# A hybrid attention/SSD kernel: one transfer per bias table, 2 KB stretches for the cumulative sums, no margin for late row sums

## The chip, the cores and the metric

The kernel runs on one core of a Trainium2 chip. The metric is the device time of one execution in microseconds (us), lower is better. Three executions of the kernel before took 1742.33, 1743.96 and 1747.86 us; the median is 1743.96 us. In the profile PE is the matrix engine (TensorE), PEld its weight loads, DVE the VectorE, ACT the ScalarE, POOL the GpSimd, and SP the engine whose queue issues nearly all DMA transfers. SPq, ACTq, DVEq mean the instruction queue of that engine.

## The reference, cut to what matters

The reference is a backbone of two layers over 256 latent tokens and 256 context tokens of width 2048, all in float32. Layer 0 joins 16 heads of neighbourhood attention with 32 heads of a bidirectional state-space scan (SSD); layer 1 is a gated short convolution. The parts that the change touches:

```python
s_lat = einsum('bqhd,bkhd->bhqk', qr, kb) * scale + bias      # bias = rpb gathered per head
s_lat = where(mask, s_lat, -inf)
...
cs = cumsum(dtc * a, axis=1)                 # a row of 128 sums per chunk, head and direction
decay = exp(where(tri, cs[:, :, None] - cs[:, None, :], -inf))
w = cb[..., None] * decay * dtc[:, None]
y = y + einsum('bign,bgrpn->bigrp', cc, h) * exp(cs)[..., None]
...
m = silu(cond) @ w + b                       # adaln: shift, scale, gate of each layer
```

The first 4096 columns of layer 0's modulation matrix are needed at once. Its last 2048 columns (the gate) and all 6144 of layer 1's are needed later; these are the "late row sums" below: 64 column blocks of 128, each in two halves of 1024 rows, so 128 products of a 128x1024 tile with a vector, each summed along its rows.

## The kernel before, in words

All large products run on PE in split precision. A weight tile of 128x1024 floats (512 KB) is loaded from DRAM into one of the `raw` buffers; ACT rounds it to its high half H (`split`, L422), DVE subtracts to get the low half Lo (`low_part`, L429), and PE multiplies act_H·H, act_H·Lo and act_L·H (`mm`, L196). There are three places for split tiles during layer 0. A tile is used up in 24 matmuls of 256 columns, or 12 or 24 of 512. PE transposes are L200.

The order of every engine's instructions is worked out while the program is built, by a planner (`Plan`, L38) that keeps a clock for each engine (`plan.t`), a ready time for each stretch of memory, and fixed costs. A DMA issue costs it 450 ns of the issuing engine; a transfer's end on the SP queue is 1000 ns, plus its bytes at 270 bytes per ns behind the transfer before, plus 1000 ns (2500 in place of the last 1000 for a transfer issued by ACT). For a DRAM tile it keeps ready times in units of 256 floats over the whole stretch from the first to the last element (`keys`, L50). Around the stream of matmuls, generators (tasks) wait in three lists, `urgent`, `side` and `back`, with horizons of 4500, 2500 and 1500 ns. Before each group of matmuls `pump` (L279) asks `may` (L247) of each task whether its next step can be put in now. For a DVE step the planner's DVE clock must be at most the horizon past PE's, and the data ready at most 400 ns past the later of the two; a step of the `back` list adds 2000 ns to the ready time first (L264).

The parts that the change touches:

- `head_gen` (L1134), one task per attention head. Its bias table of 128 rows lands in one of two tiles `bias[hd % 2]`, by three DMAs on the SP queue (L1140): 128, 64 and 128 columns at offsets 0, 304 and 544. DVE adds the window mask to the three pieces (L1146). The first score block reads columns 0 to 207 and 128 to 335, the second 336 to 543 and 464 to 671 (L1163), with zeros between, written once by POOL (L994).
- `dt_gen` (L1264) makes the cumulative sums of 64 rows (32 heads, two directions) of 256. ACT's queue writes them to DRAM as `csr` and their exponentials as `exr` (L1352, L1353), each [64, 256], direction-major. `make_x` (L1418) reads `exr` back spread over 64 partitions (L1482), `group_gen` (L1502) `csr` over 128 partitions (L1523). A head's row is two stretches of 1 KB, 32 rows apart.
- `gemv_gen` (L872), a `back` task, does the 128 late row sums. Their tiles (`in_adaT`) are loaded into `raw` buffers beside the weight tiles by `issue` (L367, the DMA at L383), at most one or two at a time. Each is one DVE instruction (L885) against `csb`, a vector spread over all partitions (L879, loaded six times). A sum is only put in when its tile is planned to be ready 1500 ns before the planner's DVE clock (L881). The sum frees the buffer, and `issue` puts the next load on the SP queue. After 32, 96 and 128 sums `n_back` rises to 3, 11.5 and 15; layer 0's residual waits for the first, layer 1's input for the second, the output for the third.

SP's queue, like each engine's, runs in the order in which the planner put its instructions; an instruction that waits holds those behind it.

Of the kernel before, what the change touches and what calls it, by code (L numbers as in the profile page):

```python
# [141 lines left out]
def kernel(ctx: ExitStack, tc, x, cx, ada0, w0, adaT, w_in, w_out, sc_in, sc_out, rpb, small, const,  # L142
# [7 lines left out]
    V, S, G, T, DMA = nc.vector, nc.scalar, nc.gpsimd, nc.tensor, nc.sync  # L150
    DMA2 = nc.scalar
    plan = Plan()
    E = plan.add
# [4 lines left out]
    def drt(shape, name):  # L158
        return dr.tile(list(shape), F32, name="dram_" + name)
# [683 lines left out]
    def dot_gen():  # L843
# [8 lines left out]
        for j in DOTS:  # L852
# [16 lines left out]
            E(V.tensor_tensor(out=S_, in0=S_, in1=P_("ab0")[:, k2].unsqueeze(2).to_broadcast([128, 2, 2]), op=ALU.add))  # L869
            got.add(("S", j))  # L870

    def gemv_gen():  # L872
        yield from rows_out(csil, crow.rearrange("r (b c) -> (r b) c", c=128), 32)
        got.add("crow")
        yield when(lambda: ("S", DOTS[-1]) in got)
        for q, blocks in enumerate(GEM):
            for h in range(2):
                yield W_("SP", crow, csb)
                E(DMA.dma_start(csb, crow[0, h * 1024:(h + 1) * 1024].partition_broadcast(128)))  # L879
                for m in blocks:  # L880
                    yield when(lambda: ("gem", m, h) in RAW and plan.ready([RAW["gem", m, h][0]]) + 1500 <= plan.t["DVE"])  # L881
                    yield W_("DVE", RAW["gem", m, h][0], csb)
                    raw, _ = RAW.pop(("gem", m, h))
                    ngem[0] -= 1
                    E(V.tensor_tensor_reduce(out=raw, in0=raw, in1=csb, scale=1.0, scalar=0.0, op0=ALU.mult, op1=ALU.add,  # L885
                                             accum_out=gp[:, h, m:m + 1]))
                    give_raw(raw)
                    issue()
            yield W_("DVE", gp)
            p2 = lambda lo, n: (gp[:, 0, lo:lo + n], gp[:, 1, lo:lo + n])  # L890
            if q == 1:
                a, b = p2(16, 32)
                o = M1.rearrange("p r b -> p (r b)")
                E(V.tensor_tensor(out=o, in0=a, in1=b, op=ALU.add))
                E(V.tensor_tensor(out=o, in0=o, in1=P_("ab1")[:, 0:32], op=ALU.add))
            else:
                a, b = p2(0 if q == 0 else 48, 16)
                E(V.tensor_tensor(out=a, in0=a, in1=b, op=ALU.add))
                E(V.tensor_tensor(out=a, in0=a, in1=P_("ab0" if q == 0 else "ab1")[:, 32:48], op=ALU.add))
                yield from rows_out(a, in_rows(mrow[q // 2]))  # L900
            n_back[0] = (3, 11.5, 15)[q]
# [89 lines left out]

    vd = drt([256, 512], "vd")
    for b_ in bias:
        E(G.memset(b_.rearrange("p a b -> p (a b)")[:, 128:544], 0.0))  # L994
    dcol = P_("dcol")


# [136 lines left out]
    def head_gen(a, h):  # L1134
# [1 line left out]
        bt, s4 = bias[hd % 2], s4s[hd % 4]  # L1136
        yield when(lambda: hd < 2 or ("pv", hd - 2) in got)
        yield W_("SP")
        bf = bt.rearrange("p a b -> p (a b)")[:, :672]
        for o_, c_, n_ in ((0, 0, 128), (304, 128, 64), (544, 192, 128)):  # L1140
            E(DMA.dma_start(bf[:, o_:o_ + n_], rpb[hd, :, c_:c_ + n_]))
        yield W_("DVE", bt)
        for o_, m_ in ((0, mask[:, 0:32]), (304, mid), (544, mask[:, 32:64])):
            n_ = m_.shape[-1]
            bv = bf[:, o_:o_ + 4 * n_].rearrange("p (c r) -> p c r", r=4)
            E(V.tensor_tensor(out=bv, in0=bv, in1=m_.unsqueeze(2).to_broadcast([128, n_, 4]), op=ALU.add))  # L1146
# [12 lines left out]
        def top(qt, ps):  # L1159
            sp = sps[qt] = tmp()  # L1160
            if qt == 0:
                E(V.memset(sp[:, 416:480], 0.0))
            b_ = bass.AP(tensor=bf.tensor, offset=bf[:, 336 * qt:].offset, ap=[bf.ap[0], [128, 2], [1, 208]])  # L1163
            sc = sp[:, span(qt)]
            E(V.tensor_tensor_reduce(out=two(sc), in0=two(ps[:, :416]), in1=b_, scale=1.0,
                                     scalar=-3.0e38, op0=ALU.add, op1=ALU.max, accum_out=s4[:, qt:qt + 1]))
            give(free_b, ps)
            E(V.tensor_scalar(out=s4[:, 2 + qt:3 + qt], in0=s4[:, qt:qt + 1], scalar1=-1.0, scalar2=None, op0=ALU.mult))
            yield W_("ACT", sp, s4)
            E(S.activation(sc, sc, AF.Exp, bias=s4[:, 2 + qt:3 + qt], scale=1.0, accum_out=s4[:, 4 + qt:5 + qt]))  # L1170
# [88 lines left out]

    dtl, csl, wst, wl = st([128, 2, 64], "dtl"), st([128, 2, 64], "csl"), st([128, 2, 64], "wst"), st([128, 64], "wl")  # L1260
    ncs, ebc = st([128, 2, 64], "ncs"), st([128, 64], "ebc")
    csr, exr = drt([64, 256], "csr"), drt([64, 256], "exr")

    def dt_gen(ps):  # L1264
        f, b = slice(0, 32), slice(32, 64)
# [83 lines left out]
        E(S.activation(rw[:64, 256:512], pr[:64, :256], AF.Exp))  # L1349
        give(free_b, pr)  # L1350
        yield W_("AQ", rw)
        E(DMA2.dma_start(csr, rw[:64, 0:256]))  # L1352
        E(DMA2.dma_start(exr, rw[:64, 256:512]))  # L1353
        give(free_t, rw)
        got.add("dt")

# [61 lines left out]
    def make_x(s, gi, ps):  # L1418
# [11 lines left out]
        if True:  # L1430
# [45 lines left out]
            for b in range(2):  # L1476
                i = 2 * gi + b
                yield W_("SP", exr)
                Et = tmp()
                for hh in range(2):  # L1480
                    e0 = exr[4 * g + 2 * b + hh, :]
                    E(DMA.dma_start(two(Et)[64 * hh:64 * hh + 64],  # L1482
                                    bass.AP(tensor=e0.tensor, offset=e0.offset, ap=[[0, 64], [32 * 256, 2], [1, 256]])))
                yield W_("PE", h1t, nb=1)
                pin = bank()
                for d_ in range(2):
                    for c in range(2):
                        hs = h0t if c == d_ else h1t
                        mm(pin[:, d_ * 256 + c * 128:d_ * 256 + (c + 1) * 128], hs[:, d_ * 256 + b * 128:d_ * 256 + (b + 1) * 128],
                           Cl[:, gi, c * 128:(c + 1) * 128], d_ == 0 and c == 0, True)  # L1490
                yield W_("DVE", pin, Et)
                E(V.tensor_tensor(out=Et, in0=pin, in1=Et, op=ALU.mult))
                give(free_b, pin)
                yield W_("DVE", Et)
                E(V.scalar_tensor_tensor(out=yi[:, i, :], in0=xf[b][:, 0:256], scalar=dcol[:, 4 * s + i:4 * s + i + 1],
                                         in1=Et[:, 0:256], op0=ALU.mult, op1=ALU.add))
                E(V.tensor_tensor(out=yi[:, i, :], in0=yi[:, i, :], in1=Et[:, 256:512], op=ALU.add))
                give(free_t, Et, xf[b])
# [3 lines left out]
    def group_gen(s, gi):  # L1502
# [14 lines left out]
        for b in range(2):  # L1517
            yield W_("SP", csr)
            rows = []
            for hh in range(2):  # L1520
                rw = tmp()
                r0 = csr[4 * g + 2 * b + hh, :]
                E(DMA.dma_start(two(rw), bass.AP(tensor=r0.tensor, offset=r0.offset, ap=[[0, 128], [32 * 256, 2], [1, 256]])))  # L1523
                rows.append(rw)
            for hh in range(2):
                h = 4 * g + 2 * b + hh
                rw = rows[hh]
                Dm, M = rw[:, 0:256], rw[:, 256:512]
                yield W_("ACT", rw)
                for c in range(2):  # L1530
                    cc = slice(c * 128, (c + 1) * 128)
                    E(S.activation(M[:, cc], M[:, cc], AF.Identity, bias=ncs[:, c, 32 + h:33 + h], scale=1.0))
                yield W_("DVE", M)
                for c in range(2):
                    cc = slice(c * 128, (c + 1) * 128)
                    E(V.scalar_tensor_tensor(out=Dm[:, cc], in0=Dm[:, cc], scalar=csl[:, c, h:h + 1], in1=M[:, cc],
                                             op0=ALU.subtract, op1=ALU.min))
                yield W_("ACT", Dm)
                E(S.activation(Dm, Dm, AF.Exp))
                for c in range(2):  # L1540
                    cc = slice(c * 128, (c + 1) * 128)
                    E(S.activation(M[:, cc], CB[:, 256 + c * 128:256 + (c + 1) * 128], AF.Copy,
                                   scale=dtl[:, c, 32 + h:33 + h]))
                yield W_("DVE", M)
                for c in range(2):
                    cc = slice(c * 128, (c + 1) * 128)
                    E(V.scalar_tensor_tensor(out=M[:, cc], in0=CB[:, cc], scalar=dtl[:, c, h:h + 1], in1=M[:, cc],  # L1547
                                             op0=ALU.mult, op1=ALU.add))
                yield W_("DVE", M, Dm)

                o = rows[0][:, hh * 256:hh * 256 + 256]
                E(V.tensor_tensor(out=o, in0=Dm, in1=M, op=ALU.mult))
                Ds.append(o)
            give(free_t, rows[1])
            if b:
                give(free_t, CB)
            both_rows.append(rows[0])
# [656 lines left out]
```

## Time and profile before

| what | value |
|---|---|
| median of three executions | 1743.96 us (1742.33 to 1747.86) |
| the profiled execution | 1743.12 us, of which its span is 1741.3 us |
| instructions | 24796 |
| ACT, DVE busy | 776.8 us (45%), 1251.3 us (72%) |
| PE granted clock | 0.999 of full speed |
| moved by DMA | 390.52 MB in 198872 packets, 224 GB/s on average |
| packets under 512 B, under 2 KB | 18712, 58456 |

The page of the profile gives the busy time of each engine, the chain of work that ended last, the costliest groups of instructions and the DMA issues with their time from issue to landing. A group's row reads: line, engine, operation, out<-in, count, then busy us and mean ns. The view of waits gives, for an engine and line, what ended its idle time: total us, number of times, longest. The table of windows gives busy us of each engine per stretch of the span, with the number of instructions, the granted clock of PE, the share of the 16 DMA engines' time that was busy, and GB/s.

### The profile page before, as it was taken

Reading aid. Unit: us, or ns where it says so; the run is one execution under the profiler, and the core shown is the slowest. Engines: PE = TensorE matmul, PEld = TensorE weight load, DVE = VectorE, ACT = ScalarE, POOL = GpSimd, SP = SyncE. Lnnn points to the kernel's source line nnn. Section 1 sums busy time; section 2 is a strip of 40 time slices with the busy share of each in tenths; the row PEclk is TensorE's granted clock in tenths of the full one; section 3 lists DMA queues with packets and bytes.
Section 4 is the critical chain, followed back from the end, with each engine's and each line's share of the span. In section 5 each row is a group of like instructions: output and inputs, shape, how many; then the busy total and the mean of one; then the engine's idle time right before and its main releaser. Section 6 shows DMA issues by size and latency. Waiting matters only on the chain.

```text
span 1741.3 us, 24796 instructions
## 1 busy us (share of the span) xinstructions
PE 1718.7 (99%) x9237; PEld 1450.3 (83%) x9237; DVE 1251.3 (72%) x2106; ACT 776.8 (45%) x1367; POOL 33.9 (2%) x28
## 2 busy tenths in 40 slices
PE   6999999999999999999999999999999999999998
PEld 4777988888888889888888898888888888888887
DVE  5698788867575878475878587887667667676754
ACT  5434544445243445243435243665445344444442
POOL 0000100001000001000001000000000000000000
PEclk9999999999999999999999999999999999999999
DMA  9987644676654765654776567757867878787863
GB/s 360 373 325 271 206 134 150 195 210 195 201 170 140 229 205 180 205 170 139 229 208 199 177 196 235 249 195 258 292 209 246 280 258 266 263 282 257 286 214 113
DMA packets 198872, 390.52 MB, mean 224 GB/s; under 512 B 18712, under 2 KB 58456, under 8 KB 198496
## 3 DMA queue, kind: packets, MB, share of 16 engines
q1 hardware_dynamic: 191472, 382.35, 67.5%
q10 hardware_dynamic: 7280, 6.59, 1.1%
q8 instruction: 72, 1.18, 0.3%
q14 instruction: 48, 0.39, 0.1%
HBM read 379.27 MB, written 9.62 MB: 223 GB/s over the span
## 4 chain that ended last, share of the span: by engine, by line
PE 94%; DMA 3%; DVE 2%; ACT 0%; issue 0%; SPq 0%; POOL 0%; DVEq 0%; ACTq 0%
PE bank L196 91%; PE bank L200 3%; DMA raw<-in_ada 1%; DMA tmp<-dram_mixd 1%; DMA csb<-dram_crow 1%; DVE w L429 0%; DMA bias<-in_rpb 0%; DVE csb L859 0%; DVE raw L885 0%; DVE mix L1704 0%; DVE tmp L1547 0%; SPq L603 0%; SPq L383 0%; DVE raw L859 0%; DVE bias L1146 0%
## 5 line engine op out<-in xcount | busy, mean ns | idle before, releaser
L422 ACT CAST w<-raw 128x1024 fp32r<-128x1024 f32 (+1 forms) x344 | 360.0, 1048 | 550.2 <-PE bank L196 415.6
L429 DVE TENSOR_TENSOR w<-raw,w 128x1024 fp32r<-128x1024 f32 (+1 forms) x344 | 416.7, 1215 | 246.3 <-ACT w L422 244.0
L196 PE MATMUL bank<-hH,w 128*128 128x256 f32 (+1 forms) x2064 | 485.6, 324 | 1.3 <-DVE w L429 1.3
L196 PE MATMUL bank<-w,hH 128*128 128x512 f32 x1280 | 406.0, 396 | 3.3 <-ACT hH L780 2.5
L196 PEld LDWEIGHTS bank<-hH,w 128*128 128x128 f32 x2064 | 344.6, 188 | 33.9 <-DVE w L429 1.9
L196 PE MATMUL bank<-hL,w 128*128 128x256 f32 (+1 forms) x1040 | 334.3, 321 | 0.0
L196 PEld LDWEIGHTS bank<-w,hH 128*128 128x128 f32 x1280 | 238.1, 189 | 55.1 <-ACT hH L780 3.0
L196 PE MATMUL bank<-w,hL 128*128 128x512 f32 x640 | 249.9, 391 | 0.2
L196 PEld LDWEIGHTS bank<-hL,w 128*128 128x128 f32 x1040 | 196.4, 189 | 14.7
L196 PE MATMUL bank<-w,h 128*128 128x512 f32 x768 | 178.5, 389 | 0.0
L196 PEld LDWEIGHTS bank<-w,h 128*128 128x128 f32 x768 | 143.9, 188 | 29.8
L885 DVE CUSTOM_DVE_ANT_0 raw<-raw,csb 128x1024 f32<-128x1024 f32 x128 | 154.9, 1216 | 0.3 <-DMA csb<-dram_crow 0.3
L196 PEld LDWEIGHTS bank<-w,hL 128*128 128x128 f32 x640 | 120.4, 188 | 25.9 <-DVE hL L792 0.9
L196 PE MATMUL bank<-w,mix 128*128 128x512 f32 x588 | 138.7, 392 | 0.6 <-DVE w L429 0.4
L196 PEld LDWEIGHTS bank<-w,mix 128*128 128x128 f32 x588 | 109.4, 188 | 23.5 <-DVE w L429 0.8
L1367 DVE SCALAR_TENSOR_TENSOR tmp<-bank,cwh,tmp 128x508 f32<-128x508 f32 (+1 forms) x96 | 71.2, 745 | 1.9
L196 PE MATMUL bank<-KL,h 128*128 128x512 f32 x264 | 63.8, 389 | 0.0
L429 DVE TENSOR_TENSOR KL<-raw,KL 128x1024 fp32r<-128x1024 f32 x32 | 39.1, 1223 | 28.2 <-ACT KL L422 28.0
L196 PEld LDWEIGHTS bank<-KL,h 128*128 128x128 f32 x264 | 49.5, 188 | 10.2
L196 PE MATMUL bank<-QT,h 128*128 128x512 f32 x168 | 55.6, 390 | 0.0
L196 PE MATMUL bank<-wH,h 128*128 128x512 f32 x168 | 55.3, 389 | 0.0
L429 DVE TENSOR_TENSOR wL<-raw,wH 128x1024 fp32r<-128x1024 f32 x31 | 37.9, 1222 | 20.6 <-ACT wH L422 20.6
(306 smaller groups left out, 1956.1 us busy)
## 6 DMA issues: line engine op xcount, KB each, us to landing
raw<-in_w_in SPq DMA_DIRECT2D x196, 512.0 KB, 3.8
raw<-in_adaT SPq DMA_DIRECT2D x128, 512.0 KB, 4.8
raw<-in_sc_in SPq DMA_DIRECT2D x128, 512.0 KB, 5.0
raw<-in_w_out SPq DMA_DIRECT2D x64, 512.0 KB, 4.6
raw<-in_ada SPq DMA_DIRECT2D x35, 512.0 KB, 8.0
raw<-in_sc_out SPq DMA_DIRECT2D x32, 512.0 KB, 4.4
raw<-in_w SPq DMA_DIRECT2D x16, 512.0 KB, 5.6
tmp<-dram_csr SPq DMA_DIRECT2D x32, 256.0 KB, 6.3
```

Source lines behind the costliest of these rows:

```text
L196: E(T.matmul(o, l, r, start=start, stop=stop, skip_group_check=True))
L200: E(T.transpose(o, i, ident if k == 128 else ident[:k, :k]))
L422: E(S.copy(H, v))
L429: E(V.tensor_tensor(out=Lo, in0=v, in1=H.bitcast(F32), op=ALU.subtract))
L885: E(V.tensor_tensor_reduce(out=raw, in0=raw, in1=csb, scale=1.0, scalar=0.0, op0=ALU.mult, op1=ALU.add, accum_out=gp[:, h, m:m + 1]))
L1367: E(V.scalar_tensor_tensor(out=do, in0=di, scalar=cwh[:, 32 * k + ch:32 * k + ch + 1], in1=do, op0=ALU.mult, op1=ALU.add))
```

## The change

It has three parts.

1. The bias table in DRAM becomes [16, 128, 3, 128]: the middle piece is padded with 64 zero columns, and one DMA brings the three pieces of 128 columns to offsets 0, 304 and 608 (192 KB a head in place of 160 KB in three DMAs). The zero fill reaches to column 608, and the second score block reads its two pieces 192 apart in place of 128.
2. `csr` and `exr` become [32, 2, 256], so that a head's two rows are one stretch of 512 floats (2 KB). ACT's queue writes each with two DMAs, one per direction; the 64 reads take one stretch per partition.
3. The late row sums are counted (`n_dot`). While fewer are done than the planner's PE clock divided by 9600 ns, less 22, the condition of 1500 ns is waived; the data must still meet the general rule for a `back` step.

```diff
@@ gemv_gen
+    n_dot = [0]
...
-                    yield when(lambda: ("gem", m, h) in RAW and plan.ready([RAW["gem", m, h][0]]) + 1500 <= plan.t["DVE"])
+                    yield when(lambda: ("gem", m, h) in RAW and (n_dot[0] < plan.t["PE"] / 9600.0 - 22 or plan.ready([RAW["gem", m, h][0]]) + 1500 <= plan.t["DVE"]))
...
+                    n_dot[0] += 1
...
-        E(G.memset(b_.rearrange("p a b -> p (a b)")[:, 128:544], 0.0))
+        E(G.memset(b_.rearrange("p a b -> p (a b)")[:, 128:608], 0.0))
@@ head_gen
-        bf = bt.rearrange("p a b -> p (a b)")[:, :672]
-        for o_, c_, n_ in ((0, 0, 128), (304, 128, 64), (544, 192, 128)):
-            E(DMA.dma_start(bf[:, o_:o_ + n_], rpb[hd, :, c_:c_ + n_]))
+        bf = bt.rearrange("p a b -> p (a b)")[:, :736]
+        E(DMA.dma_start(bass.AP(tensor=bf.tensor, offset=bf.offset, ap=[bf.ap[0], [304, 3], [1, 128]]), rpb[hd]))
...
-        for o_, m_ in ((0, mask[:, 0:32]), (304, mid), (544, mask[:, 32:64])):
+        for o_, m_ in ((0, mask[:, 0:32]), (304, mid), (608, mask[:, 32:64])):
...
-            b_ = bass.AP(tensor=bf.tensor, offset=bf[:, 336 * qt:].offset, ap=[bf.ap[0], [128, 2], [1, 208]])
+            b_ = bass.AP(tensor=bf.tensor, offset=bf[:, 336 * qt:].offset, ap=[bf.ap[0], [128 + 64 * qt, 2], [1, 208]])
@@ dt_gen
-    csr, exr = drt([64, 256], "csr"), drt([64, 256], "exr")
+    csr, exr = drt([32, 2, 256], "csr"), drt([32, 2, 256], "exr")
...
-        E(DMA2.dma_start(csr, rw[:64, 0:256]))
-        E(DMA2.dma_start(exr, rw[:64, 256:512]))
+        for d_ in range(2):
+            E(DMA2.dma_start(csr[:, d_, :], rw[32 * d_:32 * d_ + 32, 0:256]))
+        for d_ in range(2):
+            E(DMA2.dma_start(exr[:, d_, :], rw[32 * d_:32 * d_ + 32, 256:512]))
@@ make_x
-                    e0 = exr[4 * g + 2 * b + hh, :]
-                    E(DMA.dma_start(two(Et)[64 * hh:64 * hh + 64],
-                                    bass.AP(tensor=e0.tensor, offset=e0.offset, ap=[[0, 64], [32 * 256, 2], [1, 256]])))
+                    e0 = exr[4 * g + 2 * b + hh]
+                    E(DMA.dma_start(Et[64 * hh:64 * hh + 64], e0.rearrange("d t -> (d t)").partition_broadcast(64)))
@@ group_gen
-                r0 = csr[4 * g + 2 * b + hh, :]
-                E(DMA.dma_start(two(rw), bass.AP(tensor=r0.tensor, offset=r0.offset, ap=[[0, 128], [32 * 256, 2], [1, 256]])))
+                r0 = csr[4 * g + 2 * b + hh]
+                E(DMA.dma_start(rw, r0.rearrange("d t -> (d t)").partition_broadcast(128)))
@@ kernel (host)
-    table = np.concatenate([pick(0, kc[:32]), pick(0, kc[32:40]), pick(1, kc[24:32]), pick(1, kc[32:])], axis=2)
+    table = np.concatenate([pick(0, kc[:32]), pick(0, kc[32:40]), pick(1, kc[24:32]), np.zeros((16, 128, 64), np.float32),
+                            pick(1, kc[32:])], axis=2).reshape(16, 128, 3, 128)
```

## The prediction

> **What bounds the kernel now.** I read the page's busy line and chain of waits first, then a table of windows over the whole span, then the list of what PE waited for after 200 us.
>
> ```profile
> span 1741.3 us, 24796 instructions
> PE 1718.7 (99%) x9237; PEld 1450.3 (83%) x9237; DVE 1251.3 (72%) x2106; ACT 776.8 (45%) x1367; POOL 33.9 (2%) x28
> PE 94%; DMA 3%; DVE 2%; ACT 0%; issue 0%; SPq 0%; POOL 0%; DVEq 0%; ACTq 0%
> ```
>
> ```profile
> core 0: us, PE busy (x) PEld busy (x) DVE busy (x) ACT busy (x) POOL busy (x), PEclk, DMA share, GB/s
> 0.00:50.00 50.00, 35.38 (x264) 24.70 (x265) 29.21 (x88) 30.61 (x69) 3.18 (x10) 0.97 0.95 367
> 50.00:200.00 150.00, 148.67 (x902) 114.84 (x901) 116.76 (x195) 65.01 (x134) 2.65 (x1) 1.00 0.83 298
> 200.00:400.00 200.00, 200.00 (x1195) 176.21 (x1195) 158.99 (x310) 93.84 (x192) 4.44 (x3) 1.00 0.59 177
> 400.00:410.00 10.00, 8.68 (x72) 8.32 (x71) 8.00 (x18) 8.20 (x34) 4.50 (x2) 1.00 0.73 215
> 410.00:1100.00 690.00, 690.00 (x3926) 599.81 (x3925) 498.29 (x895) 289.41 (x558) 16.14 (x9) 1.00 0.62 192
> 1100.00:1115.00 15.00, 14.42 (x63) 11.40 (x62) 11.58 (x28) 9.74 (x21) 0.00 (x0) 1.00 0.67 228
> 1115.00:1736.00 621.00, 621.00 (x2825) 514.94 (x2825) 427.06 (x574) 279.95 (x364) 3.02 (x4) 1.00 0.75 247
> 1736.00:1741.30 5.30, 0.51 (x3) 0.08 (x1) 1.38 (x2) 0.00 (x0) 0.00 (x0) 0.98 0.13 49
> ```
>
> ```profile
> PE bank L196 <- DVE w L429: 1.7, 2, 1.3
> ```
>
> PE is the bound from 50 us to the end, at a granted clock of 1.00. It is idle 14.62 us in the first 50 us, 1.33 up to 200 us, 1.32 at 400 to 410, 0.58 at 1100 to 1115, and 4.79 in the tail while the last results go out. Nothing else is missing. The change's first transfers start at 219.7 us (the bias row below), and it leaves the tail's work as it is, so **all that it can win is 1.32 + 0.58 = 1.90 us**, plus pauses too short to show behind pipelined matmuls. The chain's 3% of DMA is no prize: the chain runs through a transfer from where PE paused, while PE was busy beside it. So the question is what becomes of two pauses, and whether new ones come.
>
> **The pause at 404 us.** The timeline around it, rows of SP, ACT, DVE and PE:
>
> ```profile
> 391.96 0.93 SPq L1523 DMA_DIRECT2D tmp<-dram_csr  x2
> 394.02 4.86 SPq L1141 DMA_DIRECT2D bias<-in_rpb  x6
> ...
> 397.67 0.70 ACT L1532 ACTIVATE tmp<-tmp,ncs 128x128 f32<-128x128 f32 x2 [2.03 <-DMA tmp<-dram_csr]
> 402.21 1.12 ACT L422 CAST w<-raw 128x1024 fp32r<-128x1024 f32 x1
> ...
> 401.60 1.21 DVE L1146 TENSOR_TENSOR bias<-bias,const 128x128 f32<-128x128 f32 x6 [1.04 <-DMA bias<-in_rpb]
> 403.94 1.22 DVE L429 TENSOR_TENSOR w<-raw,w 128x1024 fp32r<-128x1024 f32 x1
> ...
> 405.21 0.50 PE L196 MATMUL bank<-hH,w 128*128 128x256 f32 x2 [1.32 <-DVE w L429]
> ```
>
> Two heads' tables come by six issues in 4.86 us (0.81 each); the last lands at 401.6. DVE stood 1.04 us for it; the mask (L1146), a row sum and then the low half (L429) follow, and PE stands 1.32 us.
>
> **Part 1, one transfer per table.** 48 issues become 16. For size and landing:
>
> ```profile
> tmp<-dram_csr SPq DMA_DIRECT2D x32, 256.0 KB, 6.3
> tmp<-dram_mrow SPq DMA_DIRECT2D x12, 256.0 KB, 4.9
> tmp<-in_scr SPq DMA_DIRECT2D x12, 256.0 KB, 6.4
> bias<-in_rpb SPq DMA_DIRECT2D x32, 64.0 KB, 3.6
> ```
>
> ```profile
> L1141 SPq DMA_DIRECT2D bias<-in_rpb x48: 384/430/1962, 219.7 to 1146.2; - x48
> ```
>
> SP is spared 32 x 0.43 = 13.8 us over 930 us; none of it is PE's. At 394 us two issues of 0.81 take the place of six: the second starts at 394.83. A table of 192 KB lands between 3.6 us (64 KB) and 6.4 us (the slowest 256 KB); I take 4.4, two thirds of the way from 3.6 to the lightly loaded 4.9. That is 399.2, by the bounds 398.4 to 401.2. DVE asks at 401.60 - 1.04 = 400.56, so I book its wait as gone; at the slow bound 0.4 us of the gain is lost. But the low half can't move the full 1.04: it needs ACT's cast, which ends at 402.21 + 1.12 = 403.33, so it moves from 403.94 to 403.33. **Gain 0.6 us.** The 32 KB more per head are 0.5 MB of 390. The zero fill is POOL's, long before; the masks and the scores keep their sizes.
>
> **Part 2, stretches of 2 KB.** The pieces halve in number. The nearest rows are the other spreads over 128 partitions in stretches of 2 KB: 4.9 us (mrow) and 6.4 (scr, in a busier stretch of the span). So a `csr` read comes 0 to 1.4 us sooner than 6.3; I take 0.7, the middle, as it has rows on both ends. At 397.67 ACT was waiting for just that read (2.03 us), and its cast stands behind in ACT's queue, so 0.7 us sooner lets the cast end near 402.6, DVE reach the low half and end it near 403.85. PE ran dry at 405.21 - 1.32 = 403.89, so the whole pause goes: **0.6 to 1.3 us for parts 1 and 2 together**. With the price that the Trainium skill gives for small pieces (DMA: Bandwidth & Descriptors, "Why small descriptors are slow": about 3 cycles on each packet over one per 32 B), pieces of 1 KB cost 35 cycles and of 2 KB 67, so 70 against 67 for the same bytes: an estimate of 0.3 us from the 6.3, and a gain of 0.9 in place of 1.3. No row here separates the two.
>
> The writes go from two to four issues of ACT's queue, once:
>
> ```profile
> L1352 ACTq DMA_DIRECT2D dram_csr<-tmp x1: 507/507/507, 260.3 to 260.3; - x1
> L1353 ACTq DMA_DIRECT2D dram_exr<-tmp x1: 599/599/599, 260.9 to 260.9; - x1
> 268.24 0.37 ACT L1251 COPY half<-bank 128x256 f32<-128x256 f32 x1 [5.11 <-PE bank L196]
> L1027 SPq DMA_DIRECT2D dram_vd<-Vt x16: 496/587/1378, 193.1 to 1110.5; - x16
> ```
>
> 1.1 us more of ACT, just before 5.11 us in which it has nothing to do: nothing. Were that cover gone, a cast would be 1.1 us late. If the second half had to wait for the first to land, ACT would stand 2 x 2 us (2.0 is the landing of the whole write); but the interleaved writes of `vd` (L1027), the same pattern, go out 0.6 us apart, so I count no wait. The planner, though, keeps its ready times over the whole stretch, so it books the second halves behind the first: by its constants (60 + 2500 + 1000 + 121 ns each) its ACT clock moves about 7 us further here. That is order only, but it re-deals every choice after 261 us. First read is at 321 us, so no data are late.
>
> **Part 3, row sums without margin.** Windows of L885 alone (stretch, us, DVE busy us, instructions, two for a sum, granted clock, DMA share, GB/s), then SP's waits and landings of these loads:
>
> ```profile
> 166.00:210.00 44.00, 6.13 (x10) 1.00 0.61 198
> 210.00:332.00 122.00, 4.89 (x8) 1.00 0.51 154
> 332.00:900.00 568.00, 69.15 (x114) 1.00 0.62 192
> 900.00:1130.00 230.00, 29.15 (x48) 1.00 0.68 208
> 1130.00:1300.00 170.00, 12.25 (x20) 1.00 0.72 246
> 1300.00:1650.00 350.00, 34.24 (x56) 1.00 0.80 264
> ```
>
> ```profile
> SPq L383 <- DVE gp L885: 114.6, 88, 6.8
> L383 SPq DMA_DIRECT2D raw<-in_adaT x128: 327/341/730, 158.8 to 1635.7; - x128
> DMA to landing us min/median/max: 3.4/5.2/10.2
> ```
>
> The new rule allows T/9.6 - 22 sums at T: 12.6 at 332 us, 71.8 at 900, 95.7 at 1130, 113.4 at 1300. Done by then: 9 (5 of them before 210), 66, 90, 100. So the margin is waived nearly throughout, but few sums can move: about 6 ahead of 1130 us, 13 by 1300. Each is 1.2 us of DVE (69.15 / 57) and 512 KB, the same in all. Seven more in 1130 to 1300 add 3.7 MB / 170 us = 22 GB/s to 246, under the 264 that 1300 to 1650 bears without PE idling. **Worth nothing to PE by itself**, hidden under PE at 100%; its bounds are the 0.58 us at 1100 to 1115, if DVE is emptier there, and the loss in the second rival.
>
> **Sum.** Pause at 404: -0.6 to -1.3, I take -1.2; pause at 1100: 0 to -0.58, I take 0; the rest 0. The profiled execution took 1743.12 us (1.8 around its span): 1743.1 - 1.2 = 1741.9. The median of the three runs is 0.8 above it, which gives 1742.8; I predict **1742.3**, the middle. About 0.3%, 5.2 us, is what a measurement of this kernel can tell from no change; this is well within it.
>
> **Rivals.**
>
> *Re-dealt order, nothing won (1744.5).* The changed clocks of SP, ACT and DVE put the instructions in another order after 261 us, and pauses like the two come elsewhere: two or three of 0.6 to 1.3 us, 2.6 together, for the 1.2 won. For it: the two pauses left are where several late things met, so chance sets them. It also holds the case that part 3 does nothing: the general `back` rule still asks for ready + 1600 ns by the later of two clocks, so where DVE's is later, 100 ns is all that is waived.
>
> *Row sums stand at the head of DVE's queue: slower (1752).* Place: 332 to 1130 us, 81 sums. The planner books a load landed after 1.0 + 1.94 + 1.0 = 3.9 us, and the general rule adds 1.6: 5.5. The median landing is 5.2, the worst 10.2. A sum put in while DVE's clock lags now has only that; a later landing holds DVE, then the low half, then PE, and SP's next loads behind the buffer that the sum frees. The rows at 404 show the price, 1.04 us of DVE for 1.32 of PE. One in ten of 81 gives 8 x 1.3 = 10.4, less 1.2: 1752. It decides from 5 such stalls, 6.5 - 1.2 = 5.3 us. Against it: DVE stands 244 us for ACT's casts (row below) and PE paused only 1.7 for DVE in all, so single delays of a us are mostly swallowed. The Trainium skill (DMA: Bandwidth & Descriptors, "Anatomy of one DMA") says that the wait of a DMA sits on the issuing sequencer, which speaks for this rival: what waits for a late sum holds the weight loads behind it. The trace agrees, with 114.6 us in 88 waits of L383 for L885.
>
> ```profile
> DVE w L429 <- ACT w L422: 244.4, 160, 4.7
> ```
>
> *Both pauses go, and short ones too (1740).* 1.9 from 1743.1 is 1741.2, and a us of pauses that pipelining hides.
>
> **How the numbers follow.** Chances: forecast 0.50, re-dealt order 0.26, slower 0.14, both pauses 0.10. The runs shown spread from 1742.33 to 1747.86, so I take 1.6 us of noise on a median (1743.96 - 1742.33). Low end: 1740.2 - 1.6 = 1738.6. High end: 1744.5 + 1.6, and a third of the way to the slow case, 1748.2. Slower by over 0.3% (above 1749.2): the slow case, 0.14. Faster (below 1738.7): only noise on the last case, 0.05. Within: 0.81.
>
> **What would show it.** In the changed kernel's profile: 16 issues of bias, none waited for; `csr` landing nearer 4.9 than 6.3; no PE pause at 400 to 410; row sums some 6 further on at 1130 us and 113 done by 1300; PE's waits for L429 after 200 us under 1.7 us. Wrong would be PE idle of several us behind L429 with DVE idle ahead of L885 for `in_adaT` (the slow rival), or PE busy time off 1718.7 by more than 1 us, for its work is the same.

## The result, and the profile after

The changed kernel takes **1740.57 us** (median of 11 runs, 1739.93 to 1741.88) against 1743.96 us; the ratio is 0.998 [0.9971, 0.9988]. That is 1740 us, the time of the rival to which the prediction gave 0.10, and 1.7 us under its forecast. The gain of 3.4 us (1743.96 - 1740.57) is nearly three times the 1.2 that the prediction added up; that the time lies inside its range is owed to the low end, which was set by this rival less the noise, and is luck as far as the sum goes. The runs also lie closer together than before: within 2.0 us, where those of before lay within 5.5. The profiled execution took 1741.88 us, the slowest of the 11.

The page of after: span, busy time of each engine with its share and its instructions, shares of the chain that ended last.

```profile
span 1739.8 us, 24780 instructions
PE 1717.9 (99%) x9237; PEld 1451.0 (83%) x9237; DVE 1252.7 (72%) x2106; ACT 776.4 (45%) x1367; POOL 33.2 (2%) x28
PE 97%; DVE 2%; DMA 1%; issue 0%; SPq 0%; ACT 0%; POOL 0%; DVEq 0%; ACTq 0%
```

The same work on every engine; the transfer that the chain ran through (3% before) is nearly gone. The table of windows of after:

```profile
core 0: us, PE busy (x) PEld busy (x) DVE busy (x) ACT busy (x) POOL busy (x), PEclk, DMA share, GB/s
50.00:200.00 150.00, 147.18 (x885) 112.89 (x885) 115.19 (x194) 63.00 (x125) 0.59 (x1) 1.00 0.83 295
...
400.00:410.00 10.00, 10.00 (x87) 10.00 (x87) 7.19 (x13) 8.44 (x35) 3.08 (x2) 1.00 0.68 206
...
1100.00:1115.00 15.00, 15.00 (x68) 12.58 (x68) 13.72 (x32) 9.95 (x23) 0.00 (x0) 1.00 0.80 285
1115.00:1734.00 619.00, 619.00 (x2816) 513.66 (x2815) 414.23 (x551) 278.87 (x362) 3.83 (x4) 1.00 0.72 237
```

Both pauses are gone: PE is busy for all of 400 to 410 and of 1100 to 1115, and PE waits for nothing after 200 us. Between 50 and 200 us, ahead of the change's first transfer, it idled 2.82 us (150 - 147.18) against 1.33 before. So the span of this one profile shows less of the gain than the medians do.

The transfers of after: issue rows of the page, then the row of all bias issues (shortest, median and longest issue in ns, then the first and last start) and their landings.

```profile
tmp<-dram_csr SPq DMA_DIRECT2D x32, 256.0 KB, 5.0
tmp<-dram_exr SPq DMA_DIRECT2D x32, 128.0 KB, 5.1
...
dram_exr<-tmp ACTq DMA_DIRECT2D x2, 32.0 KB, 1.6
```

```profile
L1143 SPq DMA_DIRECT2D bias<-in_rpb x16: 551/594/1373, 221.7 to 1149.6; - x16
...
DVE bias L1148: 0.3, 1
...
DMA to landing us min/median/max: 3.7/4.3/5.3
```

A `csr` read lands 5.0 us after its issue (6.3 before), a bias table 4.3 us after its own. DVE waited for a table once, for 0.3 us. The timeline of after where the first pause was:

```profile
389.32 0.89 SPq L1526 DMA_DIRECT2D tmp<-dram_csr  x2
...
393.53 1.25 SPq L1143 DMA_DIRECT2D bias<-in_rpb  x2
...
399.14 0.63 DVE L1148 TENSOR_TENSOR bias<-bias,const 128x128 f32<-128x128 f32 x3
399.69 1.22 DVE L429 TENSOR_TENSOR w<-raw,w 128x1024 fp32r<-128x1024 f32 x1
```

Between 388 and 412 us the mask (L1148) waits for no table, and a low half follows it at once. This profile can't say which of three edits did it, nor whether the new order of instructions did. The experiments separate these.

### The profile page after: what moved, and what is told of

Same layout as the page of the kernel before. It is cut to its first block, busy times and chain, and to the rows that moved or that the text cites. A ratio compares the mean times of both kernels' runs of the same rounds, so it can differ in the third digit from the quotient of the medians.

```text
span 1739.8 us, 24780 instructions
## 1 busy us (share of the span) xinstructions
PE 1717.9 (99%) x9237; PEld 1451.0 (83%) x9237; DVE 1252.7 (72%) x2106; ACT 776.4 (45%) x1367; POOL 33.2 (2%) x28
## 4 chain that ended last, share of the span: by engine, by line
PE 97%; DVE 2%; DMA 1%; issue 0%; SPq 0%; ACT 0%; POOL 0%; DVEq 0%; ACTq 0%
PE bank L196 94%; PE bank L200 3%; DMA raw<-in_ada 1%; DVE csb L859 0%; DVE w L429 0%; DVE raw L859 0%; SPq L603 0%; DVE gt L818 0%; DVE yi L859 0%; DVE tmp L623 0%; DVE hL L792 0%; DVE sz L818 0%; ACT half L747 0%; SPq L383 0%; ACT x L633 0%
## 5 line engine op out<-in xcount | busy, mean ns | idle before, releaser
L429 DVE TENSOR_TENSOR w<-raw,w 128x1024 fp32r<-128x1024 f32 (+1 forms) x344 | 417.2, 1216 | 238.2 <-ACT w L422 237.0
L888 DVE CUSTOM_DVE_ANT_0 raw<-raw,csb 128x1024 f32<-128x1024 f32 x128 | 155.3, 1218 | 9.6 <-DMA raw<-in_adaT 6.7
L429 DVE TENSOR_TENSOR wL<-raw,wH 128x1024 fp32r<-128x1024 f32 x31 | 37.9, 1223 | 23.9 <-ACT wH L422 23.8
L429 DVE TENSOR_TENSOR QL<-raw,QT 128x1024 fp32r<-128x1024 f32 x32 | 39.1, 1223 | 21.5 <-ACT QT L422 21.2
```

Of the source, the lines that this page charges most:

```text
L429: E(V.tensor_tensor(out=Lo, in0=v, in1=H.bitcast(F32), op=ALU.subtract))
```

## The experiments

In the kernels marked "order of" another, the planner is told of the transfers which that other kernel issues, at their planned cost, while other transfers are really issued. So the instructions of PE, DVE and ACT come in exactly the same order, and only the transfers differ. All kernels compute the whole reference. Each time stands beside runs of the kernel before on the same chip, whose median was 1745.08 us for e1 to e4, 1744.38 for e5 to e8 and 1744.12 for e9 to e12.

| kernel | order | transfers of after | median us | ratio to before [95%] |
|---|---|---|---|---|
| e8 | after | all (the changed kernel again) | 1740.33 | 0.9978 [0.9969, 0.9987] |
| e1 | before | bias, csr, exr | 1740.31 | 0.9973 [0.9961, 0.9984] |
| e2 | after | none | 1745.63 | 1.0004 [0.9995, 1.0013] |
| e3 | its own | bias (part 1 alone) | 1747.04 | 1.0011 [1.0002, 1.0019] |
| e4 | its own | none (part 3 alone) | 1752.79 | 1.0041 [1.0029, 1.0054] |
| e5 | before | bias | 1746.19 | 1.0007 [0.9999, 1.0016] |
| e6 | before | csr, exr | 1740.64 | 0.9979 [0.9970, 0.9988] |
| e7 | of e4 | bias, csr, exr | 1744.46 | 0.9999 [0.9991, 1.0008] |
| e9 | before | csr | 1740.41 | 0.9982 [0.9973, 0.9991] |
| e10 | before | exr | 1744.04 | 1.0005 [0.9996, 1.0014] |
| e11 | before | csr, in pieces of 512 B | 1740.61 | 0.9981 [0.9972, 0.9990] |
| e12 | after | csr, exr | 1740.12 | 0.9981 [0.9972, 0.9989] |

**Order or transfers: e1, e2 and e8.** e1 issues the new transfers in the order of before, without part 3 (and with the new layouts of bias, `csr` and `exr` as in the change):

```diff
-            E(DMA.dma_start(bf[:, o_:o_ + n_], rpb[hd, :, c_:c_ + n_]))
+        DMA.dma_start(bass.AP(tensor=bf.tensor, offset=bf.offset, ap=[bf.ap[0], [304, 3], [1, 128]]), rpb[hd])
+        [plan.book("SP", [], plan.keys(bf[:, o_:o_ + n_]), 128 * n_ * 4) for o_, n_ in ((0, 128), (304, 64), (544, 128))]
...
-        E(DMA2.dma_start(csr, rw[:64, 0:256]))
-        E(DMA2.dma_start(exr, rw[:64, 256:512]))
+        [DMA2.dma_start(d_t[:, d_, :], rw[32 * d_:32 * d_ + 32, 256 * k_:256 * k_ + 256]) for k_, d_t in enumerate((csr, exr)) for d_ in range(2)]
+        [plan.book("ACT", plan.keys(rw[:64, 256 * k_:256 * k_ + 256]), plan.keys(d_t.rearrange("a b c -> a (b c)")), 64 * 256 * 4) for k_, d_t in enumerate((csr, exr))]
```

> The order of PE, DVE and ACT is that of the kernel before, instruction by instruction; only the transfers of parts 1 and 2 are the new ones (one bias transfer, csr and exr as 2 KB stretches), booked by the planner at the old costs. Part 3 is left as before. Transfers theory (the forecast's): bias lands near 4.3 us, csr near 5.0, PE's pause at 404 us goes, the one near 1110 goes or stays, so 1.3 to 3 us less than before: 1741 to 1742.7. Order theory (the gain comes from the re-dealt order): within 0.7 us of before, 1743.3 to 1744.7, with a PE pause for L429 left. Sums theory (part 3 makes the gain): as the order theory here.

e2 is its mirror, the order of after with the old layouts and transfers:

```diff
-    csr, exr = drt([32, 2, 256], "csr"), drt([32, 2, 256], "exr")
+    csr, exr = drt([64, 256], "csr"), drt([64, 256], "exr")
...
-        E(DMA.dma_start(bass.AP(tensor=bf.tensor, offset=bf.offset, ap=[bf.ap[0], [304, 3], [1, 128]]), rpb[hd]))
+        [DMA.dma_start(bf[:, 304 * i_:304 * i_ + n_], rpb[hd, :, i_, :n_]) for i_, n_ in enumerate((128, 64, 128))]; plan.book("SP", [], plan.keys(bf[:, :736]), 128 * 384 * 4)
```

> The order of PE, DVE and ACT is that of the changed kernel, but the transfers are the old ones: three bias transfers a head, csr and exr of two 1 KB pieces. Transfers theory: at least half of the 3.4 us gain is lost, 1742.3 or more, and PE pauses for L429 come back after 200 us; csr lands near 6.3 us and ACT's L1535 waits near 18 us in all. Order theory: 1740 to 1741.3, no PE pause after 200 us although csr lands late. Sums theory: as the order theory.

e8 is the changed kernel once more, without an edit.

> The changed kernel itself, beside the three above on one chip. 1740 to 1741.5. If part 3 and the re-dealt order are worth nothing to PE, e1 (order before, new transfers) stays within 0.6 us of it; a second profile shows whether PE is again without any pause after 200 us.

Measured: 1740.31, 1745.63 and 1740.33 us. The new transfers in the old order give the whole gain, and e1 even lies under the 1741 to 1742.7 us that was expected; the new order with the old transfers gives none. PE waits once after 200 us in e2, for the low half again:

```profile
PE bank L196 <- DVE w L429: 2.0, 1, 2.0
```

So part 3 and the re-dealt order are worth nothing measurable in the changed kernel, and the gain lies in the transfers of parts 1 and 2.

**Parts 1 and 3 alone, replanned: e3 and e4.** e3 holds the hunks of part 1 of the change, e4 those of part 3, each word for word as in the change:

```diff
+        E(DMA.dma_start(bass.AP(tensor=bf.tensor, offset=bf.offset, ap=[bf.ap[0], [304, 3], [1, 128]]), rpb[hd]))
```

> Part 1 alone, planned with its own costs, so the order is dealt anew. Transfers theory: the wait of DVE for the bias goes, 0.6 to 1.2 us less: 1742.7 to 1743.4. Order theory: anything from 1741 to 1746, depending on where pauses fall; the bias wait itself explains none of it. Sums theory: 1743 to 1745.

```diff
+                    yield when(lambda: ("gem", m, h) in RAW and (n_dot[0] < plan.t["PE"] / 9600.0 - 22 or plan.ready([RAW["gem", m, h][0]]) + 1500 <= plan.t["DVE"]))
```

> Part 3 alone, transfers as before; the sums run some 11 ahead at 1130 us as in the changed kernel. Transfers theory: no gain, 1743 to 1745, csr near 6.3 us, pauses for L429 remain. Order theory: 1741 to 1746, by chance. Sums theory: most of the gain, 1740.5 to 1742, with no pause for L429 after 200 us.

Measured: e3 1747.04 us, 2 us above before; e4 1752.79 us, 7.7 above. Both lie above every range that was expected of them, so none of the three theories foresaw what a new plan costs. The waits and the timeline of e4 (the SP row is of 385 to 400 us):

```profile
PE bank L196 <- DVE w L429: 8.9, 3, 8.2
DVE bias L1149 <- DMA bias<-in_rpb: 9.3, 3, 8.7
DVE raw L888 <- DMA raw<-in_adaT: 8.0, 8, 3.3
SPq L383 <- DVE gp L888: 1.6, 1, 1.6
```

```profile
394.49 0.93 SPq L1526 DMA_DIRECT2D tmp<-dram_csr  x2
...
398.69 4.88 SPq L1144 DMA_DIRECT2D bias<-in_rpb  x6
...
407.71 1.24 DVE L1149 TENSOR_TENSOR bias<-bias,const 128x128 f32<-128x128 f32 x6 [8.68 <-DMA bias<-in_rpb]
...
411.37 0.80 PE L196 MATMUL bank<-hH,w 128*128 128x256 f32 x2 [8.15 <-DVE w L429]
```

This is the time that the slow rival named, but only a part of its mechanism. The sums do wait for their loads, 8.0 us in 8, and PE doesn't stand for these waits. It stands 8.15 us in one piece: the six issues of two tables start 4.7 us later than in before (398.69 against 394.02), they are held on top of that (one takes 1.66 us), and DVE stands 8.68 us for them. Ahead of them in SP's queue stands a row-sum load that waited 1.6 us for the buffer of a sum, the queueing that this rival named too; old `csr` reads stand ahead as well. No run says how much of the delay each of these made.

**The same order as e4 with quick transfers: e7.** The hunks of part 3, and the transfers of e1 booked at the old costs:

```diff
+    n_dot = [0]
...
+        DMA.dma_start(bass.AP(tensor=bf.tensor, offset=bf.offset, ap=[bf.ap[0], [304, 3], [1, 128]]), rpb[hd])
```

> The order of e4 (part 3 alone) on PE, DVE and ACT, with the new transfers of parts 1 and 2. If e4's loss is one pause of 8.15 us for the old bias transfers at 400 us, and not the sums at the head of DVE's queue: the pause goes or shrinks under 1.5 us, and the time is 1740 to 1743. If the sums themselves cost PE: 1747 or more, with DVE idle ahead of L888.

Measured: 1744.46 us, between the two ranges expected, and in the waits of e7

```profile
PE bank L196 <- DVE w L429: 3.4, 2, 3.0
DVE bias L1149 <- DMA bias<-in_rpb: 5.6, 3, 4.3
```

Of e4's loss the transfers take back 7.6 us: e4 was 7.7 above the runs of before beside it, e7 is 0.1 above its own. The order keeps 4.1 (1744.46 - 1740.33 of e8, on the same chip): a table issued that late is waited for even when it comes quickly. So this order is worse, and the changed kernel's order is not. Part 3 is in both, so it is how the planner's choices fell that decides.

**Which transfer: e5, e6, e9, e10 and e12.** All keep an order and exchange one transfer. e5 takes the bias transfer alone, as e1 has it; e6 the rows alone, `csr` and `exr` as e1 has them; e9 and e10 split the rows:

```diff
-    csr, exr = drt([64, 256], "csr"), drt([64, 256], "exr")
+    csr, exr = drt([32, 2, 256], "csr"), drt([64, 256], "exr")
...
-                r0 = csr[4 * g + 2 * b + hh, :]
-                E(DMA.dma_start(two(rw), bass.AP(tensor=r0.tensor, offset=r0.offset, ap=[[0, 128], [32 * 256, 2], [1, 256]])))
+                r0 = csr[4 * g + 2 * b + hh]
+                E(DMA.dma_start(rw, r0.rearrange("d t -> (d t)").partition_broadcast(128)))
```

e12 is the changed kernel with three bias transfers a head, in the line that e2 shows.

> The order of before on PE, DVE and ACT, the transfers of before but for part 1: one bias transfer a head. If the bias transfer carries the gain: DVE no longer waits for it at 400 us, PE's pause there goes from 1.3 us to 0.7 or less (the cast on ACT, behind a csr read, then holds the low half), 1.5 to 4 us under before, and the times of the runs lie closer together. If the csr stretches carry it: within 1 us of before.

> The order of before on PE, DVE and ACT, the transfers of before but for part 2: csr and exr as stretches of 2 KB, three bias transfers a head. If the bias transfer carries the gain: within 1 us of before, DVE still waits about 1 us for the bias at 400 us, csr lands near 5.0 us. If the csr stretches carry it: 1.5 to 4 us under before, and the bias lands early enough because the reads ahead of it in the queue are shorter.

> The order of before; of the transfers only the 32 csr reads (128 partitions) are stretches of 2 KB. If the csr reads ahead of the bias in SP's queue are what makes it late: all or nearly all of e6's gain, 3 to 4.5 us under before, no PE pause at 400 us, csr near 4.9 us. If exr is needed too: 1.5 to 3 us.

> The order of before; of the transfers only the 32 exr reads (64 partitions) are stretches of 2 KB. If the csr reads make the bias late: within 1 us of before, PE still pausing for L429 at 400 us, as exr is read at other times. If any saving of engine time on the queue does it: 1 us or more under before.

> The changed kernel with its order and its csr and exr, but three bias transfers a head. If part 1 is worth nothing once csr is quick: within 0.7 us of the changed kernel, 1739.8 to 1741.3, DVE waiting under 0.5 us for the bias. If part 1 is needed in this order: 1742 or more, with a PE pause for L429 at 400 us.

Measured: in the orders of before and after, every kernel with the new `csr` takes 1740.1 to 1740.6 us. Bias alone (1746.19; the interval of its ratio includes 1) and `exr` alone (1744.04) win nothing. e9, with nothing new but 32 `csr` reads and their one write, has the whole gain. The timeline of e9 around 400 us, to be read beside that of before in the prediction:

```profile
379.11 0.42 SPq L879 DMA_DIRECT2D csb<-dram_crow  x1
...
391.00 0.89 SPq L1523 DMA_DIRECT2D tmp<-dram_csr  x2
...
393.06 2.80 SPq L1141 DMA_DIRECT2D bias<-in_rpb  x6
...
395.36 0.68 ACT L1532 ACTIVATE tmp<-tmp,ncs 128x128 f32<-128x128 f32 x2
399.89 1.12 ACT L422 CAST w<-raw 128x1024 fp32r<-128x1024 f32 x1
...
398.39 1.18 DVE L1146 TENSOR_TENSOR bias<-bias,const 128x128 f32<-128x128 f32 x6 [0.16 <-DMA bias<-in_rpb]
...
401.40 1.22 DVE L429 TENSOR_TENSOR w<-raw,w 128x1024 fp32r<-128x1024 f32 x1
```

The same six bias issues take 2.80 us instead of 4.86. The source view of the bias DMAs issued between 388 and 404 us says where the rest was; per issue, shortest, median and longest ns. Of before, then of e9, then of e5:

```profile
L1141 SPq DMA_DIRECT2D bias<-in_rpb x6: 423/430/1962, 394.0 to 398.5; - x6
```

```profile
L1141 SPq DMA_DIRECT2D bias<-in_rpb x6: 423/430/433, 393.1 to 395.4; - x6
```

```profile
L1140 SPq DMA_DIRECT2D bias<-in_rpb x2: 597/1708/2818, 396.9 to 397.6; - x2
```

Before, an issue takes 0.43 us, but one of the six took 1.96 (another, in the records behind the row, 0.96). The profile names no wait for them: the time lies inside the issue, and is called a hold here. With one transfer per table (e5) it is as long, 2.82 us in one issue. The longest bias issue in this stretch took 1.48 to 2.98 us in the six kernels with the old `csr` (before, e2, e3, e4, e5, e10) and at most 0.61 us in the eight with the new one (after, e1, e6, e7, e8, e9, e11, e12). No kernel falls between.

The hold is not the only way in which the reads make PE late. Here are ACT's waits for them in the whole span, in before and then in e9, and the `csb` issue of before (e9's stands above):

```profile
ACT tmp L1532 <- DMA tmp<-dram_csr: 18.6, 10, 3.2
```

```profile
ACT tmp L1532 <- DMA tmp<-dram_csr: 9.0, 5, 2.5
```

```profile
379.10 2.37 SPq L879 DMA_DIRECT2D csb<-dram_crow  x1
```

Ahead of the pause, each matmul of e9 starts 0.40 us later in its span than the same one of before, so a row of e9 is to be read 0.40 us earlier to compare it with before. Read so, ACT's cast, which the low half needs, comes 2.72 us sooner in e9 (402.21 and 399.89). No bias transfer stands ahead of it: ACT waited 2.03 us for a `csr` read in before (397.67), and for none here in e9. So there are two ways. Without the hold alone, the low half would still have waited for the cast, until 403.33 in place of 403.94, which is 0.6 us. With ACT alone on time, DVE would still have stood for the table, and the low half would have begun at 403.94 as before. Both are estimates from these rows; no run separates the two. Both also begin earlier: the four reads issued from 375.95 us land after 7.2 us in the median (4.7 in e9), and the `csb` issue behind them takes 2.37 us (0.42 in e9). By the next two reads, SP is 1.36 us late against PE (391.96 and 391.00).

**How much PE won, and where.** Since the orders are identical, the n-th matmul of one kernel is the n-th of the other. The difference of their start times, set to zero at 200 us, is what was lost or won up to there:

```
start of the n-th matmul, us later (+) or earlier (-) than in the profile named
                          at 400    410    1100   1115   1735
e9  csr          - before   0.00  -1.86   -1.61  -2.78  -2.79
e11 csr, 512 B   - before   0.00  -1.86   -1.61  -2.79  -2.81
e6  csr, exr     - before   0.00  -1.87   -1.88  -3.05  -3.05
e1  all three    - before   0.00  -1.86   -1.35  -2.52  -2.52
e10 exr          - before   0.00  -0.48   -0.47  +0.22  +0.19
e5  bias         - before  -0.07  +3.77   +4.02  +4.41  +4.41
e2  all old      - after    0.00  +3.75   +4.37  +4.37  +4.37
e8  nothing      - after    0.00   0.00   +0.25  +0.25  +0.25
```

The gain arises in two places and nowhere else: 1.86 us at 400 to 410 and 1.17 us at 1100 to 1115, 3.03 together. (The steps of 0.25 near 600 us also come between two runs of one kernel, as e8 shows.) From the profiled 1743.12 us that gives 1740.1. The two rows with the old `csr` beside before, e5 and e10, differ from it at these same places, by up to 4 us; that before's spread of 5.5 us also comes from there is likely, but not shown, as each kernel has one profile.

The view of busy time showed only 1.32 + 0.58 for the same two. Where the rest hid can be seen at the second one, in the timelines of PE, first of before and then of e9:

```profile
1103.42 9.01 PE L196 MATMUL bank<-w,mix 128*128 128x512 f32 x37
1112.86 1.43 PE L196 MATMUL bank<-w,mix 128*128 128x512 f32 x5 [0.43 <-DVE w L429]
```

```profile
1102.22 11.06 PE L196 MATMUL bank<-w,mix 128*128 128x512 f32 x48
```

In e9, 48 matmuls take 11.06 us: 0.39 for the last (the time of one alone) and 0.227 for each of the 47 ahead. At that pace 37 take 8.56 (36 x 0.227 + 0.39); before they took 9.01, so 0.45 us of stalling counts as busy there. What was late there, from the waits of before between 1095 and 1116 us:

```profile
ACT tmp L1532 <- DMA tmp<-dram_csr: 2.3, 1, 2.3
ACT mix L1702 <- DMA tmp<-dram_mixd: 3.3, 3, 1.7
```

ACT waits for a `csr` read, and then for reads of `mixd`; e9 shows no wait for `mixd` between 1080 and 1113 us. The place is another, the pattern the same: a late read, and a hold behind it, here on ACT's queue. Of the twelve `mixd` issues the ninth takes 1.64 us in before, 2.22 in e10 and 2.79 in e5, and at most 0.38 in e1, e6, e9 and e11, which have the same order and the new `csr`.

**Length of the stretch or place of the pieces: e11.** A read of `csr` in four pieces of 512 B, 640 B apart, in place of one of 2 KB:

```diff
-    csr, exr = drt([64, 256], "csr"), drt([64, 256], "exr")
+    csr, exr = drt([32, 4, 160], "csr"), drt([64, 256], "exr")
...
-                E(DMA.dma_start(two(rw), bass.AP(tensor=r0.tensor, offset=r0.offset, ap=[[0, 128], [32 * 256, 2], [1, 256]])))
+                E(DMA.dma_start(four(rw), bass.AP(tensor=r0.tensor, offset=r0.offset, ap=[[0, 128], [160, 4], [1, 128]])))
```

> The order of before; the csr reads are cut into four pieces of 512 B a partition in place of two of 1 KB, all else as before. If the length of the stretch sets how late the bias lands: csr lands at 8 us or later in the median, DVE waits longer for the bias at 400 us and PE pauses there for 4 us or more; 1747 to 1756. If the pause hangs on something else in the new layout: within 1 us of before.

Measured: 1740.61 us, the full gain, which neither range expected, with more packets than before had (198872). The page and the landings of `csr` in e11:

```profile
DMA packets 207144, 390.52 MB, mean 225 GB/s; under 512 B 18728, under 2 KB 66728, under 8 KB 206768
DMA to landing us min/median/max: 4.1/5.2/6.7
```

and the landings in before, then in e9:

```profile
DMA to landing us min/median/max: 5.0/6.3/10.0
```

```profile
DMA to landing us min/median/max: 4.0/4.8/6.1
```

Pieces half as long as the old ones land 1.1 us sooner than these. So it isn't the length of the stretch that made the old reads slow. What the quick layouts have in common is that a head's pieces lie beside each other, while the old ones lay 32 KB apart (32 rows of 1 KB). That distance is the cause is inferred from this; pieces of 1 KB beside each other, or other distances, were not tried. Against it speak the `exr` reads, of the same two pieces 32 KB apart, over 64 partitions. Their median landing, in before and then in e10, which lays the pieces side by side:

```profile
tmp<-dram_exr SPq DMA_DIRECT2D x32, 128.0 KB, 4.6
```

```profile
tmp<-dram_exr SPq DMA_DIRECT2D x32, 128.0 KB, 4.7
```

So the distance alone doesn't make a read slow, and what does in the `csr` reads stays open. Parts 1 and 2 without part 3 were not run: the planner finds no order for them, and stops where layer 1's input needs the 96 sums. To that extent part 3 does serve: it lets an order exist.

## Why the prediction was right, and where it was wrong

- **The bound, "all that it can win is 1.32 + 0.58 = 1.90 us, plus pauses too short to show"**: the two places were right, the size was not. They held 3.03 us (1.86 and 1.17). The prediction named what pipelined matmuls hide, and then summed it as zero outside of one rival.
- **Part 1, "two issues of 0.81 take the place of six: the second starts at 394.83"**: this step failed. 0.81 was a mean of issues of 0.43 and of two that were held. The hold doesn't go with the number of issues: e5 spent 3.47 us on two. The 0.6 us booked for part 1 was nothing (e5 1.0007 [0.9999, 1.0016]; e12 without part 1 0.9981, e8 with it 0.9978). The landing of 4.4 us was right: 4.3. At its slow bound of 401.2, 0.4 us of the gain would have been left (401.60 - 401.2), not lost.
- **Part 2, "I take 0.7"**: the path by ACT's cast was right, the size was not. A `csr` read came 1.3 us sooner in the median of all, at the upper end of 0 to 1.4, but the two at the pause landed 2.3 us sooner (6.7 in before, 4.4 in e9) and went out 1.36 sooner, and the cast came 2.72 us sooner. Only the landing of one read was counted; the four reads before it, and the issues held behind the reads, were not. Here lies nearly all that was mis-sized: the term was 0.6 beside part 1's 0.6, and was 3.0 alone (e9). The rule on small pieces was no help. The Trainium skill (DMA: Bandwidth & Descriptors, "Why small descriptors are slow") makes the same bytes cost more in smaller pieces, which gave 0.3 us sooner; by it e11 would have been the slowest of the three layouts, and its landing contradicts that: 5.2 us against 6.3.
- **"Pause at 1100: 0 to -0.58, I take 0"**: it went, and by `csr` alone (e9). The prediction looked at DVE's load there and not at what ACT waited for.
- **The ACT writes, at nothing**: right. The second `exr` write went out 0.5 us after the first, and both landed in 1.6 us.
- **Part 3, "worth nothing to PE by itself"**: right for the changed kernel (e1 without it 1740.31, e8 with it 1740.33). The sums moved further than forecast. Windows of L888 in after, two instructions to a sum:

```profile
166.00:210.00 44.00, 6.14 (x10) 1.00 0.67 216
210.00:332.00 122.00, 3.59 (x6) 1.00 0.49 147
332.00:900.00 568.00, 79.84 (x131) 1.00 0.64 200
900.00:1130.00 230.00, 32.35 (x54) 1.00 0.69 219
1130.00:1300.00 170.00, 13.48 (x22) 1.00 0.72 247
```

  100 are done by 1130 us (201 / 2), 10 ahead of the 90 before, where 6 were forecast; 111 by 1300, where 113 were.
- **Sums at the head of DVE's queue, 1752**: in after they wait 6.7 us in 9 for their loads, 1.6 at the longest, and PE never pauses for it. Alone, part 3 did give 1752.79, for the most part by another mechanism, late tables; that the times agree is luck. The prediction priced the sums' own stalls. It named SP's loads behind the buffer of a sum, but put no price on a table standing behind them. The rival of the re-dealt order, with 2.6 us of new pauses, was the nearer idea, and e4's order cost more than that even with quick rows (4.1).
- **What would show it**: 16 issues of bias, `csr` nearer 4.9, no pause at 400 to 410, waits for L429 under 1.7 us (none), PE busy within 1 us (0.8): all came, but for one table waited for (0.3 us). Half of the forecast gain had been credited to part 1, which gave none of it.

## What to carry to other kernels

A late read's price is more than one wait: follow it through the engine that waits for it, look back to the reads before it, and look at what the same queue issues next. Read the longest issue beside the median, since a mean hides one that was held. Where two kernels run the same instructions in the same order, compare them matmul by matmul; this finds all of a pause, where the idle time of a pipelined engine shows a part. Before an order dealt anew by a planner is blamed or praised, fix the order and exchange the transfers.

## What had not been expected of the hardware

The same 2 KB of DRAM, read into each of 128 partitions (256 KB), lands after 6.3 us in two pieces of 1 KB that lie 32 KB apart, after 5.2 in four pieces of 512 B, 640 B apart, and after 4.8 in one piece. By the DMA packet records the 8192 old packets of 1 KB took some 72 ns each, an estimate: all packets of this size take 2081 us together in before and 1491 in e9, where these are missing, and the others are taken to be as quick in both. The median packet of 1 KB takes 46. The 16512 packets of 512 B that e11 adds took 30 ns each by the same reckoning, near that size's median of 27. This makes an old read 256 x 72 = 18.4 us of engine time, one of e11 512 x 30 = 15.4; shared by 16 DMA engines they differ by 0.2 us, so most of the 1.1 us at landing isn't packet time, and what it is stays open. The second surprise was the queue: an issue on SP that takes 0.43 us took 1.5 to 3.0 us behind two such reads, in every profile that has them ahead of the bias issues at 388 to 404 us, and in none that doesn't. ACT's queue showed the same after 1090 us (1.64 us and more, against 0.37). Elsewhere in the span single bias issues of up to 1.37 us occur with the new layout too (the row of after), so other things hold an issue as well; what holds it no run shows.
